# Moving weight loads and casts inside the attention layer of a two-layer decoder trunk

## The chip, the cores and the metric

The kernel runs on one core of a Trainium2 chip. The metric is the device time of one execution in microseconds (us). PE is the matrix engine, DVE the vector engine, ACT the scalar engine, POOL the general one, and SP issues most of the DMAs.

## What is computed

The reference is a trunk of two residual layers over 1024 positions of width 1024, with a final RMS norm. The first layer is a gated linear recurrence; the second, in which the change lies, is causal attention with a forget term, 16 heads of 64:

```python
h = rms_norm(x, norm_g[1])
u = h @ w_in                                  # q, k, v, gate, forget logits
cum = cumsum(log_sigmoid(f_logit + b_f))
logits = q @ k.T / 8 + (cum[q] - cum[k])      # causal
o = softmax(logits) @ v
x = x + (o * silu(gate)) @ w_out
```

All products are done at about float32 precision: each operand is split into a high and a low half, and three matmuls (high x high, low x high, high x low) make one product.

## The kernel before

**Tiling.** In the attention layer the heads come in pairs (128 columns). Each pair needs a K, a Q and a gate (G) projection; each is a *unit* of two halves of 512 positions, and a half is 24 matmuls into one PSUM bank (`gps`), in four steps of six (`gemm_steps`, line 137). Every four heads need 256 columns of V: a *value phase* of 192 matmuls (`vps`), `values`, line 695. The first value group is made before the heads start; groups one to three follow heads 3, 7 and 11.

**Weights.** A unit's weights are two tiles of 128x512 float32, a value group's are four (`in_wv`). SP loads each tile into one of three buffers `wf` (`loaded`, line 114). The cast (`cast16`, line 641) makes the halves in fp16: ACT writes the high half, DVE the low one (line 647), and with that the buffer is free again. The fp16 tiles have eight buffers.

**Scores.** `maxima` (line 925) makes four score blocks of 128 positions for a head and a half `c`: PE writes S; DVE masks it and takes the maximum (line 949); ACT takes the exponential (`p`); DVE the reciprocal of its sum; ACT and DVE write the normalised halves (`pp`, line 963); SP issues a transposing DMA (`pT`, line 966). `weigh` (line 972) multiplies with V into O. `pieces` (line 807) copies K and Q of the head after next into T and U.

**Order.** `run` (line 1018) follows a string for each half of a head: a digit is a step of `weigh` or `maxima`, a dot a step of the *fill*, which plays units (`play`, line 677). At step 0 of a unit's first half `play` loads the next unit's weights and at step 2 of its last half it casts both tiles, behind the last exponential so far (`seen[0]`). When a value phase is due, `run` calls the generator `values` before order places 2 and 5 and at the last score block; after the string the matmuls of the phase run. Each engine's final order is made by a scheduler from these hints, and each engine, SP's queue too, works in its order. The units of the K projection of pairs 3, 5 and 7 are split by a value phase, and their weights are loaded and cast a second time for the second half.

Of the kernel before, what the change touches and what calls it, by code (L numbers as in the profile page):

```python
# [22 lines left out]
KT = 8  # L23
# [12 lines left out]
def f32(ap):  # L36
    return ap.bitcast(F32)
# [3 lines left out]
def trunk(ctx: ExitStack, tc: tile.TileContext, xt, w0, wg, wo0, pc, gn, gf, w1, wv, wf, bf, wo1, out):  # L41
# [26 lines left out]
    def matmul(*args, **kw):  # L68
        pe[0] = nc.tensor.matmul(*args, **kw)  # L69
        return pe[0]  # L70
# [82 lines left out]
    def take(gen, n):  # L153
        for _ in range(n):
            next(gen, None)
# [43 lines left out]
    with nullcontext(ExitStack()) as l0:  # L199
# [8 lines left out]
        def pair():  # L208
            return tuple(hpool.tile([P, HALF], F32R, tag=t, name=t) for t in ("hh", "hl"))
# [33 lines left out]
        first = ([], [])  # L243
        early = [weights(w0[0], lo_eng=nc.vector), weights(w0[NB], lo_eng=nc.gpsimd)]
        k = 0
# [11 lines left out]
        raw = [[pair() for k in range(KT)] for h in range(2)]  # L257
# [321 lines left out]
        for h, cs in enumerate(halves):  # L579
# [4 lines left out]
            for d0 in range(0, KT, 4):  # L584
# [6 lines left out]
                for db, o in enumerate(pts, d0):  # L591
                    mm3(o, wl[db][1], y[1], False, True)
                    x = xs[h][db]
# [26 lines left out]
    with ExitStack() as l1:  # L620
# [11 lines left out]
        seen = [None]  # L632

        def load16(src, shape, b):

            wt = loaded(shape)
            for part, sl in src:
                fetch(wt[:, :, sl], part)
            return wt, b

        def cast16(wt, b):

            n = wt.shape[1]
            both = wpool.tile([P, 2, *wt.shape[1:]], FP16, tag=next(slots), name="w16")
            hi, lo = both[:, 0], both[:, 1]
            cast_last[0] = nc.scalar.activation(hi, wt, AF.Copy, scale=scales[:, b : b + 1])
            nc.vector.scalar_tensor_tensor(lo, wt, scales[:, b : b + 1], hi, ALU.mult, ALU.subtract)  # L647
            return [(hi[:, k], lo[:, k]) for k in range(n)]
# [4 lines left out]
        class Weights:  # L653

            def __init__(self, b):
                self.b, self.raw, self.parts = b, None, None

            def load(self):
                if self.raw is None:
# [1 line left out]
                        load16([(w1[self.b][:, k : k + 4], slice(0, P))], (4, P), 4 + self.b) for k in range(0, KT, 4)  # L661
                    ]

            def cast(self):
                self.load()
                if self.parts is None:
                    self.parts = [x for r in self.raw for x in cast16(*r)]
                return self.parts

        plan = []  # L670

        def job(w, h, start, use):
            u = dict(w=w, h=h, start=start, use=use)
            plan.append(u)
            return u

        def play(units):

            for u in units:
                u["start"]()  # L680
                w, h = u["w"], u["h"]
                after_ = [v["w"] for v in plan[plan.index(u) + 1 :] if v["w"] is not w][:1]
                pt = ps.tile([P, HALF], F32, tag="g", name="gps1")
                for i, _ in enumerate(gemm_steps(pt, zip(w.cast(), hT[h]))):
                    for v in after_ if seen[0] is not None else ():
                        if h == u["first"] and i == 0:
                            v.load()
                        if h == u["last"] and i == 2:
                            with tc.issue_after(seen[0].ins):
                                v.cast()  # L690
                    yield
                nc.vector.scalar_tensor_tensor(pt, pt, unit_w[:, 4 + w.b : 5 + w.b], rs1[h], ALU.mult, ALU.mult)
                u["use"](h, pt)

        def values(g):

            ex = HEADS if g == 0 else 0
            parts, raw = [], []
            for k in range(0, KT, 2):
                src = [(wv[g, :, k : k + 2], slice(0, 256))]  # L700
                if ex:
                    src.append((wf[:, k : k + 2], slice(256, 256 + ex)))
                raw.append(load16(src, (2, 256 + ex), g))
                if k == 2 and not ex:
                    yield
                if k % 4 == 0:
                    continue
                with tc.issue_after(seen[0].ins) if k == 2 and not ex else nullcontext():
                    parts += [x for r in raw for x in cast16(*r)]
                raw = []  # L710
                if k == 2 or not ex:
                    yield
            Vs[2 * g], Vs[2 * g + 1] = [], []
            todo = [(st, k) for st in range(8) for k in range(KT)]
            if not ex:

                todo[: 2 * KT] = [(st, k) for h in range(2) for st in range(2) for k in range(h * 4, h * 4 + 4)]
            pts = {}
            for st, k in todo:
                if k == 0:  # L720
                    if st % 2:
                        pt = ps.tile([P, SEQ], F32, tag="S", name="vps")[:, : 256 + ex]
                    else:
                        pt = ps.tile([P, 256 + ex], F32, tag="g", name="vps")
                    pts[st] = pt
                pt = pts[st]
                c = (st % 4) * P
                xh, xl = hT[st // 4][k]
                wh, wl = parts[k]
                xh, xl = xh[:, c : c + P], xl[:, c : c + P]  # L730
                matmul(pt, xh, wh, start=k == 0, stop=False)
                matmul(pt, xl, wh, start=False, stop=False)
                matmul(pt, xh, wl, start=False, stop=k == KT - 1)
                if k % 4 == 1:
                    yield
                if k < KT - 1:
                    continue
                if ex and st < 4:
                    take(splitting, 2)
                if True:  # L740
                    if ex:
                        nc.vector.tensor_scalar(fz[:, st], pt[:, 256:], rf[:, st : st + 1], None, ALU.mult)
                    for a in range(2):
                        v = vpool.tile([P, 4, HD], FP16, tag=f"v{st}", name=f"v{st}", bufs=2)
                        src = pt[:, a * P : (a + 1) * P].rearrange("p (b d) -> p b d", b=2)
                        rv_ = rv[:, g, st : st + 1]
                        to_hi(v[:, 0::3], src, nc.scalar, scale=rv_)
                        nc.vector.scalar_tensor_tensor(v[:, 1:3], src, rv_, v[:, 0::3], ALU.mult, ALU.subtract)
                        Vs[2 * g + a].append(v)
# [10 lines left out]
        def kq_units(pair, parts):  # L760

            units = []
            for is_k, hs in parts:
                if hs[0] == 0 or pair == 0 or is_k and pair in (3, 5, 7):
                    kqw[is_k] = Weights(is_k * 8 + pair)

                def start(is_k=is_k, first=[True]):
                    if is_k not in kq:
                        kq[is_k] = tuple(
                            kqpool.tile([P, SEQ], F32R, tag=f"qk{p}{is_k}", name=f"qk{p}") for p in "hl"  # L770
                        )

                def use(h, pt, is_k=is_k):
                    cs = halves[h]
                    hi, lo = kq[is_k]
                    if is_k:
                        to_hi(hi[:, cs], pt, nc.scalar)
                        to_lo(lo[:, cs], pt, hi[:, cs], nc.vector)
                    else:
                        to_hi(hi[:, cs], pt, nc.scalar, scale=0.125)  # L780
                        nc.vector.scalar_tensor_tensor(lo[:, cs], pt, 0.125, f32(hi[:, cs]), ALU.mult, ALU.subtract)

                new = [job(kqw[is_k], h, start, use) for h in hs]
                for u in new:
                    u["first"], u["last"] = hs[0], hs[-1]
                units += new
            return units

# [83 lines left out]
        first = values(0)  # L872
# [145 lines left out]
        def run(order, *gens, fill=iter(()), side=iter(()), vals=None):  # L1018

            for n, i in enumerate(order):  # L1020
                if vals and n in (2, 5):
                    with tc.issue_after(turns[-1].ins):
                        next(vals)
                if vals and n == order.rfind("1"):
                    next(vals)
                    behind[:] = loaded_last[0], cast_last[0]
                with tc.issue_after(pe[0].ins):
                    next(fill if i == "." else gens[int(i)], None)
                if i == ".":
                    next(side, None)  # L1030
            for g in gens:
                drain(g)
# [201 lines left out]
        for hd in range(HEADS):  # L1234
            pair = hd // 2
# [21 lines left out]
            first, second = LAST if hd > 11 else ORDER  # L1257
            if hd == HEADS - 1:
                first = "1..1.0.1.0.1..."
# [12 lines left out]
            vals = values(hd // 4 + 1) if hd % 4 == 3 and hd < 12 else None  # L1272
# [91 lines left out]
```

## Time and profile before

| | |
|---|---|
| time, median of 3 runs | 1081.03 us (1080.33 to 1084.85) |
| profiled execution | 1080.8 us, its span 1079.0 us |
| busy | PE 95%, DVE 73%, ACT 61%, POOL 9% |
| transfers | 148.92 MB, 138 GB/s over the span |
| score blocks (S) of the 16 heads | 506.7 to 1037.0 us |
| value phases after heads 3, 7, 11 | from 625.23, 756.33 and 887.66 us |

Busy time is an average over both layers. What a wait of PE costs is read from the timeline: a row there is a group of equal instructions with its start and duration in us, and in brackets the idle time of its engine before it and what ended that. PE's matmuls overlap, so that 24 of them take less than 24 times the duration of one. The granted clock is the share of full speed at which PE may run.

### The profile page before, as it was taken

The page shows a single profiled execution, that of the slowest core. Times are in us where ns is not written, and L with a number is a line of the kernel's source. Part 1 is how long each engine was busy: PE and PEld are TensorE (multiplying, and loading weights), DVE is VectorE, ACT ScalarE, POOL GpSimd, SP SyncE. Part 2 cuts the span into 40 slices and gives each one's busy share as a digit, 9 for nine tenths or more (in the row PEclk, how much of TensorE's full clock was granted, in tenths as well). Part 3 has the DMA queues.
Part 4 walks back from the last instruction along what each step waited for, and adds up shares of the span by engine and source line. Part 5 has one row for each costly group of instructions (what it writes and reads, how often), then busy time and mean ns, then how long its engine had stood idle before and what let it go on. Part 6 is the DMA issues. An engine that isn't in the chain of part 4 may idle for free. (4 is left out here: it accounts for less than half of the span.)

```text
span 1079.0 us, 15071 instructions
## 1 busy us (share of the span) xinstructions
PE 1030.3 (95%) x5094; PEld 722.4 (67%) x5094; DVE 784.9 (73%) x1456; ACT 662.3 (61%) x1211; POOL 92.5 (9%) x87
## 2 busy tenths in 40 slices
PE   9999999999999999998899989999899998999997
PEld 6787878888888888664455465454754546477676
DVE  7789657656956698976878847788387873886675
ACT  8469665656565664757656646666376663764455
POOL 1311011113121110000000000000000000012110
PEclk9999999999999999999999999999999999999999
DMA  6112324233423312534779964978569994689984
GB/s 241 60 49 70 117 88 132 90 106 98 132 84 112 98 56 75 162 96 110 157 155 183 182 160 92 194 165 179 137 111 190 167 185 113 144 185 235 256 200 157
DMA packets 219805, 148.92 MB, mean 138 GB/s; under 512 B 161936, under 2 KB 174864, under 8 KB 219728
## 3 DMA queue, kind: packets, MB, share of 16 engines
q1 hardware_dynamic: 217328, 140.09, 53.7%
q0 software_dynamic: 2400, 7.87, 2.4%
q8 instruction: 40, 0.66, 0.3%
q14 instruction: 37, 0.30, 0.1%
HBM read 73.33 MB, written 11.67 MB: 79 GB/s over the span
## 5 line engine op out<-in xcount | busy, mean ns | idle before, releaser
L69 PE MATMUL gps<-h,w 128*128 128x512 f16 x1152 | 274.5, 384 | 15.5 <-DVE w L647 12.1
L69 PEld LDWEIGHTS <-w 128*128 128x128 f16 x1152 | 105.0, 99 | 145.5 <-issue 17.3
L57 ACT ACTIVATE p<-S,m 128x128 f32<-128x128 f32 (+7 forms) x128 | 94.7, 740 | 72.4 <-DVE m L949 43.1
L57 ACT ACTIVATE pp<-p,sums 128x128 f16<-128x128 f32 (+7 forms) x128 | 96.1, 771 | 36.3 <-DVE sums L961 13.2
L963 DVE SCALAR_TENSOR_TENSOR pp<-p,sums,pp 128x128 f16<-128x128 f32 (+7 forms) x128 | 102.1, 813 | 15.4 <-ACT pp L57 14.7
L69 PE MATMUL S<-T,U 96*128 96x512 f32 (+7 forms) x384 | 108.6, 392 | 2.6 <-ACT p L57 2.2
L69 PE MATMUL vps<-w,h 128*128 128x256 f16 (+1 forms) x768 | 90.5, 277 | 17.9 <-ACT w L57 10.8
L949 DVE CUSTOM_DVE_ANT_0 S<-S,mask 128x128 f32<-128x128 f32 (+7 forms) x128 | 96.9, 759 | 7.9 <-PE S L69 7.3
L110 POOL TENSOR_TENSOR wl<-wf,wh 128x512 fp32r<-128x512 f32 x46 | 71.2, 1552 | 323.1 <-ACT wh L57 264.9
L69 PEld LDWEIGHTS <-h 128*128 128x128 f16 x768 | 75.3, 99 | 32.7 <-issue 14.2
L69 PEld LDWEIGHTS S<-T,U 128*128 128x128 f32 (+1 forms) x384 | 68.9, 191 | 23.9 <-ACT p L57 7.0
L57 ACT CAST wh<-wf 128x512 fp32r<-128x512 f32 x88 | 51.7, 594 | 51.9 <-PE ops L69 26.8
L647 DVE SCALAR_TENSOR_TENSOR w<-wf,wsq,w 128x512 f16<-128x512 f32 (+1 forms) x74 | 54.1, 749 | 33.8 <-ACT w L57 33.6
L69 PE MATMUL ops<-yh,wh 128*128 128x512 f32 x192 | 76.6, 399 | 0.6 <-ACT yh L57 0.5
L69 PE MATMUL ups<-hh,wh 128*128 128x512 f32 x192 | 76.1, 397 | 0.9 <-ACT hh L57 0.8
L69 PE MATMUL ups<-hh,wl 128*128 128x512 f32 x192 | 75.7, 394 | 1.2 <-POOL wl L110 1.2
L69 PE MATMUL ups<-hl,wh 128*128 128x512 f32 x192 | 76.2, 397 | 0.1
L69 PE MATMUL gps<-hh,wh 128*128 128x512 f32 x192 | 75.7, 394 | 0.4 <-ACT wh L57 0.4
L69 PE MATMUL ops<-yh,wl 128*128 128x512 f32 x192 | 75.7, 394 | 0.1
L69 PE MATMUL gps<-hh,wl 128*128 128x512 f32 x192 | 75.5, 393 | 0.0
L69 PE MATMUL gps<-hl,wh 128*128 128x512 f32 x192 | 75.5, 393 | 0.0
L69 PE MATMUL ops<-yl,wh 128*128 128x512 f32 x192 | 74.5, 394 | 0.0
(196 smaller groups left out, 1899.1 us busy)
## 6 DMA issues: line engine op xcount, KB each, us to landing
wf<-in_w SPq DMA_DIRECT2D x106, 256.0 KB
wsf<-in_w SPq DMA_DIRECT2D x48, 256.0 KB
wf<-in_wo SPq DMA_DIRECT2D x64, 128.0 KB
T<-qkh SPq DMA_DIRECT2D x64, 128.0 KB
U<-qkh SPq DMA_DIRECT2D x64, 128.0 KB
x<-in_xt SPq DMA_DIRECT2D x16, 256.0 KB
wsf<-in_wv SPq DMA_DIRECT2D x16, 256.0 KB
x1d<-x SPq DMA_DIRECT2D x16, 256.0 KB
```

The costliest lines, as they stand in the source:

```text
L57: act[0] = op(*args, **kw)
L69: pe[0] = nc.tensor.matmul(*args, **kw)
L110: return eng.tensor_tensor(lo, src, f32(hi), ALU.subtract)
L647: nc.vector.scalar_tensor_tensor(lo, wt, scales[:, b : b + 1], hi, ALU.mult, ALU.subtract)
L949: nc.vector.tensor_tensor_reduce(S[:, :n], S[:, :n], mask[:, SEQ - n :], -1.0, -NEG, ALU.add, ALU.min, accum_out=m)
L963: nc.vector.scalar_tensor_tensor(both[:, :, 1], p, r, both[:, :, 0], ALU.mult, ALU.subtract)
```

## The change

There are three edits. In `values` the first three of the four value tiles of groups one to three are loaded together, before order place 1; the first two are cast before place 5, then the fourth is loaded, and at the last score block the last two are cast. In `play` the next unit's two tiles are cast at steps 1 and 2 (one each) rather than both at step 2. For the K unit that is played just ahead of a value phase the next unit's load moves from step 0 to step 2 and its casts to steps 2 and 3.

```diff
-            def cast(self):
+            def cast(self, n=2):
                 self.load()
-                if self.parts is None:
-                    self.parts = [x for r in self.raw for x in cast16(*r)]
+                while len(self.parts) < 4 * n:
+                    self.parts += cast16(*self.raw[len(self.parts) // 4])
                 return self.parts
...
-            u = dict(w=w, h=h, start=start, use=use)
+            u = dict(w=w, h=h, start=start, use=use, load=0, cast=(1, 2))
...
-                        if h == u["first"] and i == 0:
+                        if h == u["first"] and i == u["load"]:
                             v.load()
-                        if h == u["last"] and i == 2:
+                        if h == u["last"] and i in u["cast"]:
                             with tc.issue_after(seen[0].ins):
-                                v.cast()
+                                v.cast(u["cast"].index(i) + 1)
...
+            else:
+                for k in range(0, 6, 2):
+                    load_v(k)
+                yield
+                with tc.issue_after(seen[0].ins):
+                    cast_v(2)
+                load_v(6)
+                yield
+                cast_v(2)
+                yield
...
+                    if is_k and hs == (0,) and pair in (3, 5, 7):
+                        u["load"], u["cast"] = 2, (2, 3)
...
-                if vals and n in (2, 5):
+                if vals and n in (1, 5):
```

`load_v(k)` loads one value tile (`load16`), `cast_v(n)` casts the next n that are loaded. What the scheduler makes of it is shown at three places.

First ACT ahead of head 11's K unit (`w` are the unit's two fp16 tiles, `pp` the normalised scores, `p` the exponentials). Before:

```order
L57 ACTIVATE p,sums<-S,m 128x1024
L57 ACTIVATE pp<-p,sums 128x7x128
L57 ACTIVATE pp<-p,sums 128x8x128
L57 ACTIVATE yo<-O,wsq 64x512
L57 ACTIVATE p,sums<-S,m 128x128
L57 ACTIVATE w_8098<-wf,wsq 128x512
L57 ACTIVATE w_8101<-wf,wsq 128x512
```

Of the change:

```order
L57 ACTIVATE p,sums<-S,m 128x1024
L57 ACTIVATE w_8065<-wf,wsq 128x512
L57 ACTIVATE pp<-p,sums 128x7x128
L57 ACTIVATE pp<-p,sums 128x8x128
L57 ACTIVATE yo<-O,wsq 64x512
L57 ACTIVATE p,sums<-S,m 128x128
L57 ACTIVATE w_8107<-wf,wsq 128x512
```

The first cast moved ahead of the two normalising activations, the second stayed. DVE's low halves moved in the same way, and the same holds in the other odd heads.

Second SP's queue at the third value phase (`in_wv` value tiles, `in_w` the next unit's, `T` and `U` the copies of K and Q). Before:

```order
L966 DMA_TRANSPOSE pT<-pp 128x2x128
L66 DMA wf<-in_wv 128x512 x2
L966 DMA_TRANSPOSE pT<-pp 128x4x128
L66 DMA wf<-in_w 128x512
L966 DMA_TRANSPOSE pT<-pp 128x6x128
L66 DMA T_4062<-cumd 2x512
L66 DMA T_4062<-qkh 64x512
L66 DMA wf<-in_w 128x512
L66 DMA wf<-in_wv 128x512
```

The fourth value tile comes six rows later. Of the change:

```order
L982 DMA_TRANSPOSE pT<-pp 128x2x128
L66 DMA wf<-in_wv 128x512 x3
L982 DMA_TRANSPOSE pT<-pp 128x4x128
L982 DMA_TRANSPOSE pT<-pp 128x6x128
L66 DMA wf<-in_wv 128x512
L66 DMA T_4062<-cumd 2x512
L66 DMA T_4062<-qkh 64x512
L982 DMA_TRANSPOSE pT<-pp 128x8x128
L66 DMA T_4062<-qkh 64x512
L66 DMA T_4062<-qkl 64x512
L66 DMA wf<-in_w 128x512 x3
```

The first value load stands behind the same transpose as before; the unit's loads moved behind all four value tiles.

Third ACT in the same phase, from the value casts (`w_8144`, `w_8147`, `w_8170` and `w_8173` before, with the unit's `w_8203` and `w_8206` among them) to the copies out of PSUM (`v`). Before:

```order
L57 ACTIVATE w_8144<-wf,wsq 128x512
L57 ACTIVATE w_8147<-wf,wsq 128x512
L57 ACTIVATE w_8170<-wf,wsq 128x512
L57 ACTIVATE w_8203<-wf,wsq 128x512
L57 ACTIVATE w_8173<-wf,wsq 128x512
L57 ACTIVATE w_8206<-wf,wsq 128x512
L57 ACTIVATE yo<-O,wsq 64x512
L57 ACTIVATE v_8276<-vps,rv 128x2x64
L57 ACTIVATE v_8294<-vps,rv 128x2x64
L57 ACTIVATE v_8325<-vps,rv 128x2x64
L57 ACTIVATE v_8279<-vps,rv 128x2x64
```

Of the change, where `w_8146` to `w_8169` are the value tiles:

```order
L57 ACTIVATE w_8146<-wf,wsq 128x512
L57 ACTIVATE w_8149<-wf,wsq 128x512
L57 ACTIVATE w_8166<-wf,wsq 128x512
L57 ACTIVATE w_8169<-wf,wsq 128x512
L57 ACTIVATE yo<-O,wsq 64x512
L57 ACTIVATE w_8203<-wf,wsq 128x512
L57 ACTIVATE v_8276<-vps,rv 128x2x64
L57 ACTIVATE v_8294<-vps,rv 128x2x64
L57 ACTIVATE w_8212<-wf,wsq 128x512
L57 ACTIVATE v_8325<-vps,rv 128x2x64
L57 ACTIVATE v_8279<-vps,rv 128x2x64
```

`v_8276` and `v_8279` are the two copies of the first of the eight blocks, `v_8294` and `v_8325` the first copies of the second and third. The unit's casts moved behind the value tiles and stand among the copies. PE has the same matmuls in both kernels. Of the 192 of a phase the first that needs the third value tile is the 49th before and the 41st now; for the fourth tile it is the 73rd before and the 54th now. The first four blocks are complete after 84, 88, 92 and 96 matmuls before, and after 65, 69, 80 and 96 now.

More of the change, by code (lines that the diff above doesn't have):

```diff
@@ L655, in __init__ @@
             def __init__(self, b):
-                self.b, self.raw, self.parts = b, None, None
+                self.b, self.raw, self.parts = b, None, []
             def load(self):
@@ L698, in values, with load_v @@
             parts, raw = [], []
-            for k in range(0, KT, 2):
+            def load_v(k):
                 src = [(wv[g, :, k : k + 2], slice(0, 256))]
@@ L703, in values, with cast_v @@
                 raw.append(load16(src, (2, 256 + ex), g))
[L704 to L712, printed above, removed]
+            def cast_v(n=1):
+                for _ in range(n):
+                    parts.extend(cast16(*raw.pop(0)))
+            if ex:
+                for k in range(0, KT, 2):
+                    load_v(k)
+                    if k % 4:
+                        cast_v(2)
+                    if k == 2:
+                        yield
+            else:
+                for k in range(0, 6, 2):
+                    load_v(k)
+                yield
[3 more added lines that the diff above has]
+                yield
+                cast_v(2)
+                yield
             Vs[2 * g], Vs[2 * g + 1] = [], []
```

## The prediction

> **What bounds the kernel now.** I read the page first, then the list of waits for PE, then the timeline around the longest of these waits, and last the short windows that show the granted clock.
>
> ```profile
> span 1079.0 us, 15071 instructions
> PE 1030.3 (95%) x5094; PEld 722.4 (67%) x5094; DVE 784.9 (73%) x1456; ACT 662.3 (61%) x1211; POOL 92.5 (9%) x87
> ```
>
> PE is busy for 1030.3 of 1079.0 us. The order printed for the changed kernel holds the same matmuls, so the change can only move PE's idle time and the clock at which PE runs. In the list of waits for PE each row gives total, count and longest, in us:
>
> ```profile
> PE gps L69 <- DVE w L647: 12.1, 8, 2.0
> PE vps L69 <- ACT w L57: 10.8, 8, 2.1
> PE vps L69 <- DVE v L748: 7.0, 6, 1.8
> ...
> PE gps L69 <- ACT w L57: 2.2, 2, 1.9
> PE O L69 <- DMA pT<-pp: 2.0, 2, 1.6
> ```
>
> Two kinds of wait concern the change. In a **value phase** (`vps`: 192 matmuls in a row, three times after the first group) PE waits for cast value tiles, and once for the PSUM copies (L748). At the start of a **unit** (`gps`) it waits for the cast of the unit's own weights. The third value phase shows the first kind; columns are start, duration, engine, line, operation, and in brackets the idle time before it with what ended it:
>
> ```profile
> 882.90 1.05 SPq L66 DMA_DIRECT2D wf<-in_wv  x2
> 886.67 1.37 ACT L57 ACTIVATE w<-wf,wsq 128x512 f16<-128x512 f32 x2 [0.24 <-DMA wf<-in_wv]
> 887.66 5.40 PE L69 MATMUL vps<-w,h 128*128 128x256 f16 x48
> 888.75 0.95 SPq L66 DMA_DIRECT2D wf<-in_w  x1
> 889.80 0.38 SPq L66 DMA_DIRECT2D wf<-in_wv  x1
> 894.04 1.34 ACT L57 ACTIVATE w<-wf,wsq 128x512 f16<-128x512 f32 x2 [6.00 <-DMA wf<-in_wv]
> 894.82 2.78 PE L69 MATMUL vps<-w,h 128*128 128x256 f16 x24 [1.75 <-ACT w L57]
> 895.58 0.33 SPq L66 DMA_DIRECT2D wf<-in_wv  x1
> 898.70 1.34 ACT L57 ACTIVATE w<-wf,wsq 128x512 f16<-128x512 f32 x2 [3.31 <-DMA wf<-in_wv]
> 899.47 2.78 PE L69 MATMUL vps<-w,h 128*128 128x256 f16 x24 [1.87 <-ACT w L57]
> 903.47 2.79 PE L69 MATMUL vps<-w,h 128*128 128x256 f16 x24 [1.22 <-DVE v L748]
> ```
>
> ACT sits idle 6.00 and 3.31 us for value tiles three and four, because their loads were issued only at 889.80 and 895.58: with three load buffers they stood behind the next unit's tiles. The other two phases:
>
> ```profile
> 625.23 5.40 PE L69 MATMUL vps<-w,h 128*128 128x256 f16 x48 [1.55 <-ACT w L57]
> 632.62 4.45 PE L69 MATMUL vps<-w,h 128*128 128x256 f16 x24 [1.99 <-ACT w L57]
> 637.23 2.78 PE L69 MATMUL vps<-w,h 128*128 128x256 f16 x24 [0.16 <-ACT w L57]
> 641.23 10.65 PE L69 MATMUL vps<-w,h 128*128 128x256 f16 x96 [1.22 <-DVE v L748]
> ```
>
> ```profile
> 756.33 5.40 PE L69 MATMUL vps<-w,h 128*128 128x256 f16 x48 [0.58 <-ACT w L57]
> 762.50 2.78 PE L69 MATMUL vps<-w,h 128*128 128x256 f16 x24 [0.77 <-ACT w L57]
> 767.39 2.78 PE L69 MATMUL vps<-w,h 128*128 128x256 f16 x24 [2.11 <-ACT w L57]
> 771.39 3.77 PE L69 MATMUL vps<-w,h 128*128 128x256 f16 x33 [1.22 <-DVE v L748]
> ```
>
> The 24 matmuls at 632.62 took 4.45 us where others take 2.78. The windows tell why; after the span come PE's busy time and, further on, the granted clock:
>
> ```profile
> 629.91:633.32 3.41, 1.42 (x14) 1.11 (x13) 0.71 (x2) 1.34 (x2) 0.00 (x0) 1.00 0.66 169
> 633.32:636.74 3.42, 3.42 (x19) 2.44 (x17) 0.70 (x2) 0.29 (x1) 0.00 (x0) 0.50 0.69 153
> 896.15:899.56 3.41, 1.54 (x15) 1.24 (x13) 0.17 (x2) 0.86 (x2) 0.00 (x0) 1.00 0.86 199
> 899.56:902.98 3.42, 2.69 (x24) 2.16 (x23) 3.36 (x7) 2.83 (x8) 0.00 (x0) 1.00 0.77 237
> ```
>
> A stretch of 3.41 us in which PE is busy for only 1.42 us is followed by 3.42 us at half clock; one with 1.54 us is not. So idle time of about 2 us inside one such stretch costs a second time.
>
> **Value phases: what goes.** The waits after each phase's start are, with 4.45 - 2.78 = 1.67 for the half clock: first 1.99 + 1.67 + 0.16 + 1.22 = 5.04, second 0.77 + 2.11 + 1.22 = 4.10, third 1.75 + 1.87 + 1.22 = 4.84. Together 14.0 us.
>
> **Value phases: what comes.** Tiles one to three are now issued together, so they land one behind the other. The fourth stands next in SP's queue and waits for the buffer of tile one. The load at 888.75 waited for that same buffer, so the fourth can go at 888.75. From issue to cast the rows give 898.70 - 895.58 = 3.1 to 894.04 - 889.80 = 4.2; PE follows the cast by 894.82 - 894.04 = 0.8. That is 892.7 to 893.8. In the new PE order 53 matmuls stand ahead of the first that needs it, 53 x 5.40 / 48 = 6.0 us from 887.66: 893.6. The wait is between nothing and, should a load take 1 us longer than these, 1 us; I take 0.2 a phase, 0.6 in all. Waiting behind this load on SP are the transposed tile and the pieces of T and U, which PE needs only after the remaining matmuls.
>
> The PSUM wait does not vanish, although the first two blocks are now complete after 65 and 69 of the first 96 matmuls. On ACT the first block's second copy stands behind the cast of the next unit's second tile and behind a copy of the third block, complete after 80. With that tile loaded last (issue near 892.5, cast not before 896) the copy ends about where it did. I keep 1.1 of the 1.22 us, 3.3 in all; the ends are 0 and, if these loads come 1 us later, 6.6. The moved unit loads and casts themselves cost nothing else: the last 96 matmuls, 10.65 us, cover them, and without that cover the two casts would cost 1.34.
>
> **The start of a phase does not move.** In SP's new order the first value load stands directly behind the same transpose as before, and the first cast follows its landing (0.24 idle on ACT at 886.67 ended by the DMA). Whatever PE gains just ahead of a phase therefore turns into a longer wait at its start, with a half clock behind it where it passes 2 us. Ahead of the second and third phase PE now waits for a unit's cast:
>
> ```profile
> 747.32 1.25 PE L69 MATMUL gps<-h,w 128*128 128x512 f16 x5 [2.02 <-DVE w L647]
> 748.87 4.06 PE L69 MATMUL gps<-h,w 128*128 128x512 f16 x18
> 877.73 1.25 PE L69 MATMUL gps<-h,w 128*128 128x512 f16 x5 [2.01 <-DVE w L647]
> 879.44 5.57 PE L69 MATMUL gps<-h,w 128*128 128x512 f16 x18
> ```
>
> If these go, the second phase is awaited for 0.58 + 2.02 = 2.6 us, the third for 2.01 + 1.51 = 3.5 (5.57 - 4.06 = 1.51 is its half clock). I charge two half clocks of 1.6 us, 3.2 in all; the ends are none and three (4.8).
>
> The Trainium skill, page "TensorE: Matmul & The Clock Gate", section "Why this matters for your kernels", asks only that idle gaps stay below about 3 us. By that rule the second phase would lose no clock and the sum would be 1.6 us lower. The rows above differ: 1.99 us of idle time already brought 0.50, so the rows decide.
>
> **Units: casts one step apart.** The first cast now stands ahead of two normalising activations, so its DVE half is done before the unit starts. All ten waits of this kind (12.1 + 2.2 = 14.3 us, in eight units) have it on their path. Besides the half clock at 879.44 two more follow them:
>
> ```profile
> 694.76:698.18 3.42, 3.42 (x10) 1.42 (x9) 2.95 (x10) 0.67 (x2) 0.00 (x0) 0.50 0.92 175
> 824.47:827.88 3.41, 3.41 (x9) 1.43 (x9) 2.60 (x8) 0.40 (x1) 0.00 (x0) 0.50 1.10 225
> ```
>
> Three half clocks of 1.5 make 4.5, and 18.8 us at most. How much stays is the unknown. Three of these units stand ahead of value phases and give nothing (above). For the others the score chain on DVE and ACT must keep up:
>
> ```profile
> 701.59 0.76 DVE L692 SCALAR_TENSOR_TENSOR gps<-gps,wsq,rs 128x512 f32<-128x512 f32 x1 [1.44 <-PE gps L69]
> 726.52 2.97 PE L69 MATMUL O<-pT,v 128*128 128x512 f16 x16 [0.37 <-DMA pT<-pp]
> 833.97 0.72 ACT L57 ACTIVATE w<-wf,wsq 128x512 f16<-128x512 f32 x1 [2.47 <-DMA wf<-in_w]
> ```
>
> Behind one of them DVE waits 1.44 us for PE: so much the chain can follow. At 726.52 PE already waits for the chain's transposed tile, so no more stays. In another the chain waits for a load (833.97) and cannot follow. I count 1.44 for three of the five, 4.2 us; the ends are 0 and 18.8.
>
> **Sum.** -14.0 + 0.6 + 3.3 + 3.2 - 4.2 = -11.1. The profiled execution took 1080.8 us (span 1079.0 and 1.8 around it), close to the median of 1081.03. Forecast: 1080.8 - 11.1 = **1069.7 us**.
>
> **Rivals.**
> - *No half clock.* The waits ahead of the phases fall across two stretches, or stay short: 1069.7 - 3.2 = 1066.5. For it: stretches with 1.54 us of work did not trip. Against: 3.5 us hardly splits evenly. Chance 0.12.
> - *The unit gains stay.* PE is the only bound and all 18.8 us hold: 1080.8 - 14.0 + 0.6 + 3.3 - 18.8 = 1051.9. For it: PE's 95%. Against: the wait at 726.52. Chance 0.12.
> - *One wait takes the place of two.* The fourth tile lands late enough for a 2 us wait with its half clock in each phase, 3 x 3.6 = 10.8: 1080.8 - 14.0 + 3.3 + 10.8 - 4.2 = 1076.7. For it: the margin at 893.6 is 0.2 us or less against a slow load. Chance 0.20.
> - *Slower.* In eight heads the early cast delays the two activations behind it, by one cast on ACT (1.37 / 2 = 0.7) and one on DVE (0.7), and through them the transposed tiles that O needs. If all 1.4 us reach O, nothing of the 4.2 stays and 8 x 1.4 = 11.2 is added to -6.9: 1085.1, and 1089.6 with three half clocks. It turns the sign above 6.9 / 8 = 0.9 us a head. Against it: O waits twice in the whole kernel, 2.0 us. Chance 0.06.
> - *The change doesn't do what it says*: the loads do not start earlier at all; this is already in the forecast, as the phase's start.
>
> **How the numbers follow.** The forecast has 0.50, with 1066 to 1074 as its own range. A measurement of this kernel tells about 0.5% (5.4 us) from no change, so faster means below 1075.6. Forecast, first and second rival and a fifth of the third make 0.78 faster; the rest of the third makes 0.16 same; the fourth 0.06 slower. The range 1058 to 1079 leaves out the second rival and the fourth, 0.18.
>
> **What would show it.** Right: in the value phases the ACT waits for value tiles of 6.00 and 3.31 us shrink to one short one, of the 10.8 us of `vps` waits for ACT the 8.7 in the middle of the phases (all but 1.55 and 0.58) nearly vanish while those at the start grow to 6 to 9, the waits of `gps` for L647 nearly vanish, and the waits of S and O for the score chain grow. Wrong: a `vps` wait of 2 us in the middle of a phase (third rival), O waiting in every odd head (fourth), or value phases that begin earlier against the transpose ahead of them.

## The result and the profile after

The changed kernel takes **1066.6 us** (median of 4 runs, 1066.17 to 1067.16) beside 1082.59 of the kernel before on the same chip: ratio **0.9853**, 95% interval 0.9827 to 0.9878, about 16 us less. Its profiled execution has a span of 1065.4 us. Of all executions reported below, one of the six of the kernel with the unit loads not moved ran slow, with 1726.5 us at a granted clock of 0.557, and no ratio includes it.

```profile
span 1065.4 us, 15063 instructions
PE 1028.7 (97%) x5094; PEld 721.8 (68%) x5094; DVE 784.2 (74%) x1456; ACT 659.9 (62%) x1211; POOL 92.2 (9%) x87
```

The list of waits for PE, changed kernel (total, count, longest, in us):

```profile
PE vps L69 <- ACT w L57: 8.3, 3, 3.5
PE O L69 <- DMA pT<-pp: 6.0, 5, 2.0
PE S L69 <- ACT p L57: 4.7, 13, 1.1
```

The waits of `gps` for the units' casts are gone from it, and the waits of `vps` for ACT, eight before, are three. The timeline says which three; PE's rows of the three value phases:

```profile
625.73 10.64 PE L69 MATMUL vps<-w,h 128*128 128x256 f16 x96 [2.66 <-ACT w L57]
637.11 10.65 PE L69 MATMUL vps<-w,h 128*128 128x256 f16 x96 [0.74 <-DVE v L762]
...
750.45 12.31 PE L69 MATMUL vps<-w,h 128*128 128x256 f16 x96 [2.18 <-ACT w L57]
762.95 10.65 PE L69 MATMUL vps<-w,h 128*128 128x256 f16 x96 [0.19 <-DVE v L762]
...
878.28 23.98 PE L69 MATMUL vps<-w,h 128*128 128x256 f16 x192 [3.48 <-ACT w L57]
```

Each phase now waits once, at its start, and then runs through: 96 matmuls take 10.64 us without a break where the copies out of PSUM do not interrupt. The 12.31 and the 23.98 us (twice 10.64 is 21.3) hold half clocks, 1.67 and 2.70 us. The windows around them (span, busy time of PE, of its weight loads PEld, of DVE, ACT and POOL, granted clock, DMA share, GB/s):

```profile
747.64:751.06 3.42, 1.24 (x12) 0.97 (x11) 1.81 (x3) 1.53 (x3) 0.00 (x0) 1.00 1.03 260
751.06:754.47 3.41, 3.41 (x18) 2.37 (x17) 1.56 (x3) 0.99 (x2) 0.00 (x0) 0.50 0.88 188
873.94:877.35 3.41, 0.86 (x7) 0.55 (x6) 1.88 (x3) 0.61 (x1) 0.00 (x0) 1.00 0.54 138
877.35:880.76 3.41, 2.48 (x12) 1.72 (x12) 2.14 (x3) 2.11 (x3) 0.00 (x0) 0.50 0.94 224
880.76:884.18 3.42, 3.42 (x18) 2.35 (x16) 0.84 (x2) 1.40 (x2) 0.00 (x0) 0.50 1.00 216
```

Where the time went is read from the groups of PE's matmuls over the attention layer alone, from the first S matmul to the last (506.7 to 1037.0 us before, 508.3 to 1023.2 after). Behind the second bar stands the idle time ahead of the group. Before:

```profile
L69 PE MATMUL gps<-h,w 128*128 128x512 f16 x1034 | 248.2, 385 | 15.5 <-DVE w L647 12.1 <-ACT w L57 2.2 <-DVE qkl L781 1.2
L69 PE MATMUL S<-T,U 128*128 128x512 f32 (+2 forms) x383 | 108.3, 392 | 2.6 <-ACT p L57 2.2
L69 PE MATMUL O<-pT,v 128*128 128x512 f16 (+2 forms) x368 | 66.9, 326 | 2.1 <-DMA pT<-pp 2.0
L69 PE MATMUL vps<-w,h 128*128 128x256 f16 x576 | 66.5, 277 | 14.4 <-ACT w L57 10.8 <-DVE v L748 3.7
```

After:

```profile
L69 PE MATMUL gps<-h,w 128*128 128x512 f16 x1034 | 242.7, 380 | 1.1 <-DVE qkl L795 1.1
L69 PE MATMUL S<-T,U 96*128 96x512 f32 (+7 forms) x384 | 106.2, 385 | 5.0 <-ACT p L57 4.7
L69 PE MATMUL vps<-w,h 128*128 128x256 f16 x576 | 68.2, 284 | 9.2 <-ACT w L57 8.3 <-DVE v L762 0.9
L69 PE MATMUL O<-pT,v 128*128 128x512 f16 (+2 forms) x368 | 67.0, 326 | 6.0 <-DMA pT<-pp 6.0
```

Idle time falls from 34.6 to 21.3 us (-13.3). Half clocks fall from 6.2 us (1.67 and three of 1.51) to 4.4 (-1.8). Together -15.1; the layer became 530.3 - 514.9 = 15.4 us shorter. The span shows only 13.6, mostly because in this execution the first layer, which has no edit, ended 1.6 us later.

### The profile page after: what moved, and what is told of

The parts are those of the page before. It is cut to its first block, busy times and chain, and to the rows that moved or that the text cites. A ratio compares the mean times of both kernels' runs of the same rounds, so it can differ in the third digit from the quotient of the medians.

```text
span 1065.4 us, 15063 instructions
## 1 busy us (share of the span) xinstructions
PE 1028.7 (97%) x5094; PEld 721.8 (68%) x5094; DVE 784.2 (74%) x1456; ACT 659.9 (62%) x1211; POOL 92.2 (9%) x87
## 2 busy tenths in 40 slices
DMA packets 219805, 148.92 MB, mean 140 GB/s; under 512 B 161936, under 2 KB 174864, under 8 KB 219728
## 5 line engine op out<-in xcount | busy, mean ns | idle before, releaser
L69 PE MATMUL gps<-h,w 128*128 128x512 f16 x1152 | 269.1, 380 | 1.3 <-DVE qkl L795 1.1
L69 PE MATMUL S<-T,U 96*128 96x512 f32 (+7 forms) x384 | 106.2, 385 | 5.0 <-ACT p L57 4.7
L69 PEld LDWEIGHTS <-h 128*128 128x128 f16 x768 | 76.7, 101 | 28.0 <-issue 10.8
L69 PEld LDWEIGHTS S<-T,U 128*128 128x128 f32 (+1 forms) x384 | 67.7, 190 | 28.8 <-ACT p L57 13.6
L69 PE MATMUL O<-pT,v 128*128 128x512 f16 (+3 forms) x396 | 71.0, 322 | 6.0 <-DMA pT<-pp 6.0
```

## Experiments

Idle time by group comes from the same rows of each profile, from its first to its last S; a *half clock* is one stretch of 3.41 us at 0.50 in that layer. Ratios are against the kernel before on the same chip, in five rounds (the changed kernel's first row: the result above).

| kernel | us | ratio [95%] | gps | S | O | vps | half clocks |
|---|---|---|---|---|---|---|---|
| before (profile shown) | 1082.6 | 1 | 15.5 | 2.6 | 2.1 | 14.4 | 4 |
| changed | 1066.6 | 0.9853 [0.9827, 0.9878] | 1.1 | 5.0 | 6.0 | 9.2 | 3 |
| changed, again | 1065.3 | 0.9850 [0.9825, 0.9876] | 1.1 | 4.6 | 5.2 | 8.8 | 1 |
| value tiles only | 1069.4 | 0.9891 [0.9871, 0.9912] | 15.5 | 3.5 | 2.1 | 4.8 | 3 |
| unit casts only | 1076.1 | 0.9972 [0.9958, 0.9986] | 1.1 | 4.6 | 6.0 | 19.0 | 2 |
| unit loads not moved | 1062.7 | 0.9824 [0.9803, 0.9845] | 1.2 | 4.7 | 6.3 | 8.0 | 2 |
| value loads by POOL | 1061.9 | 0.9828 [0.9804, 0.9852] | 1.1 | 6.1 | 12.0 | 0.0 | 1 |
| early loads (0, 3) | 1054.0 | 0.9760 [0.9741, 0.9778] | 1.1 | 4.7 | 5.7 | 1.6 | 0 |
| early (0, 3), casts together | 1067.1 | 0.9874 [0.9852, 0.9896] | 15.4 | 1.3 | 2.0 | 6.7 | 3 |
| early loads (0, 2) | 1055.4 | 0.9764 [0.9743, 0.9785] | 1.1 | 4.7 | 6.2 | 2.6 | 0 |
| early (0, 2), casts together | 1059.9 | 0.9806 [0.9786, 0.9825] | 15.5 | 2.8 | 2.0 | 0.4 | 1 |
| early (0, 3), unit loads not moved | 1056.7 | 0.9773 [0.9753, 0.9793] | 1.2 | 6.5 | 7.8 | 2.5 | 0 |
| early (0, 3), shorter lag | 1059.1 | 0.9815 [0.9796, 0.9834] | 1.1 | 4.1 | 5.6 | 2.2 | 0 |
| early (0, 3), pieces by POOL | 1127.5 | 1.0415 [1.0388, 1.0443] | 1.1 | 4.6 | 62.9 | 0.5 | 17 |

### Each edit alone

Value tiles only (against the changed kernel):

```diff
-            u = dict(w=w, h=h, start=start, use=use, load=0, cast=(1, 2))
+            u = dict(w=w, h=h, start=start, use=use, load=0, cast=(2, 2))
...
-                                v.cast(u["cast"].index(i) + 1)
+                                v.cast(2)
...
-                        u["load"], u["cast"] = 2, (2, 3)
+                        u["load"], u["cast"] = 2, (3, 3)
```

> The changed kernel with both casts of a unit put back to one step (the later of its two steps); the value tiles stay as changed. Theory of the prediction (waits inside the value phases go for good; what PE gains ahead of a phase comes back as a wait for the first value tile, and what it gains ahead of other units is partly taken by the score chain): nearly the whole gain is here. The profile of the changed kernel gives the parts: 14.0 us of waits and half clock inside the three phases went, 0.74 us of the PSUM wait stayed, while of the 18.8 us of unit waits and half clocks 8.3 - 2.1 = 6.2 came back at the phase starts, 4.4 as half clock there and about 5.7 as waits of S and O. So 1082.6 - 13.3 = 1069.3 us, ratio 0.987 to 0.990, the gps waits for L647 back at 10 to 14 us, the vps waits for ACT at 2 to 3 us, no half clock inside the first value phase. Rival, the edits add up independently (each wait removed is time removed): the unit casts were worth 10 us or more of the 16.0, so this kernel keeps 6 us or less, ratio 0.994 or higher.

Unit casts only (against the kernel before; `cast(n)` as in the change):

```diff
-                        if h == u["last"] and i == 2:
+                        if h == u["last"] and i in (1, 2):
...
-                                v.cast()
+                                v.cast(i)
```

> The kernel before with the unit casts alone one step apart; the value tiles as before. Theory of the prediction: the gps waits for L647 (12.1 us) vanish, but the starts of the value phases do not move, so the vps waits for ACT grow by about 6 us at the starts, one to three half clocks of 1.6 us follow them, and S and O wait up to 6 us more for the score chain: a net gain of 1 to 5 us, ratio 0.995 to 0.999, no change that can be told by 0.5%. Rival, the edits add up independently: 10 us or more, ratio 0.991 or lower. Second rival, the early cast delays the normalising activations: slower than before, O waiting in every odd head.

The value tiles alone bring 1.09%, 11.8 us; the unit casts alone 0.28%, 3.0 us. Both numbers lie where the theory put them, and both rivals fall: the unit casts are not worth 10 us, and they do not make the kernel slower. The edits nearly add (14.8 of about 16 us); what the rival had wrong is the size of the second. The list of waits with the unit casts only shows where their 14.4 us of `gps` idle time went:

```profile
PE vps L69 <- ACT w L57: 15.3, 8, 2.7
...
PE O L69 <- DMA pT<-pp: 5.9, 6, 3.3
PE S L69 <- ACT p L57: 4.3, 12, 1.2
```

`vps` for ACT grew from 10.8 to 15.3, O from 2.0 to 5.9, S from 2.2 to 4.3: 10.5 us came back. (This execution took 1074.6 us, 1.5 less than the median, and has two half clocks less than the one before; so its rows show a larger gain than the 3.0 us of the ratio.)

### Does SP's queue hold the start of a phase?

Value loads by POOL, and early loads (both against the changed kernel):

```diff
+                loads_by[0] = nc.gpsimd
                 for k in range(0, 6, 2):
                     load_v(k)
+                loads_by[0] = nc.sync
                 yield
                 with tc.issue_after(seen[0].ins):
                     cast_v(2)
+                loads_by[0] = nc.gpsimd
                 load_v(6)
+                loads_by[0] = nc.sync
```

```diff
-                if vals and n in (1, 5):
+                if vals and n in (0, 3):
```

> The changed kernel, but the value tiles of groups one to three are loaded through POOL's queue in place of SP's; the order on all other engines stays. In the changed kernel PE waits 2.66, 2.18 and 3.48 us at the starts of the value phases for the cast of the first value tile, with 4.4 us of half clock behind the last two, and ACT is idle 1.81, 1.65 and 2.96 us ahead of those casts for the landing. Theory (the first load stands in SP's queue behind a transpose that waits for its scores): with a queue of their own the loads go as soon as their buffer is free, the first casts come earlier by what ACT is idle, 6.4 us in all, the waits at the starts fall to 0.5 to 0.9 each and the half clocks go: 1066.6 - 6.4 - 4.4 = 1055.8, up to 1062 if the score chain takes part of it. Rival, the start hangs on the free buffer or on ACT's order, not on SP's queue: the starts stay, within 2 us of the changed kernel. Second rival, POOL's queue lands its tiles later than SP's: slower than the changed kernel, with ACT waiting longer for value tiles.

> The changed kernel with the three value loads ahead of order place 0 in place of 1, and the fourth tile's load with the first two casts ahead of place 3 in place of 5; all through SP's queue. In that queue the three loads now stand ahead of the pieces of T and of the first transpose of the half, so at the third phase they can be issued near 868.7 in place of 872.63 us. Theory (SP's queue sets the start of a phase): the first cast comes earlier by the idle time of ACT ahead of it (1.81, 1.65, 2.96 us), the half clocks of 4.4 us go, the fourth tile is still in time (issue near 876 at the earliest, needed at 881): 1056 to 1062 us. Rival, what is moved behind the three loads (pieces of T, transposes) becomes late in its turn: O or S wait 2 to 3 us more in heads 4, 8 and 12, and the time stays within 3 us of the changed kernel.

Yes. With a queue of their own PE waits 0.0 us for value tiles, and with early loads 1.4. The third phase with early loads, from PE's and SP's rows:

```profile
859.80 1.81 SPq L66 DMA_DIRECT2D wf<-in_wv  x3
...
867.72 0.59 SPq L66 DMA_DIRECT2D wf<-in_wv  x1
...
865.47 5.79 PE L69 MATMUL vps<-w,h 128*128 128x256 f16 x50
871.95 15.69 PE L69 MATMUL vps<-w,h 128*128 128x256 f16 x142 [0.68 <-ACT w L57]
```

The loads go 5.7 us before PE's first matmul of the phase, against 878.28 - 872.63 = 5.65 with 3.48 us of idle PE among them in the changed kernel; the phase starts without a wait, and no stretch of the whole layer runs at half clock. The 1054.0 us are the fastest median of the study, 2 us better than the 1056 to 1062 expected and some 10 us (0.9853 to 0.9760) better than the changed kernel. In this phase PE still waits 0.68 us for the fourth tile. The rival, that what stands behind the three loads becomes late, falls (O 5.7 against 6.0, S 4.7 against 5.0).

POOL's queue removed the same wait, but its 1061.9 us are the upper end of what was expected. Its groups:

```profile
L69 PE MATMUL S<-T,U 96*128 96x512 f32 (+7 forms) x384 | 106.3, 386 | 6.1 <-ACT p L57 5.8
L69 PE MATMUL O<-pT,v 128*128 128x512 f16 (+2 forms) x368 | 68.7, 331 | 12.0 <-DMA pT<-pp 9.5 <-DMA T<-qkh 2.5
L69 PE MATMUL vps<-w,h 128*128 128x256 f16 x576 | 63.4, 273 | 0.0
```

O's idle time doubled: 2.60, 1.87 and 2.51 us of it stand directly ahead of the three phases. Ahead of the first, POOL issues value tiles at 609.70 and 615.45 us, while SP issues the last two transposes of the half between 610.75 and 616.66, and O waits for them until 620.7. With early loads SP issues these transposes from 610.29 to 615.68 and the tiles from 615.73 on, and O waits 0.2 us.

### Are the unit casts worth more when the starts can move?

Both casts of a unit back in one step (as in *value tiles only*), once with `n in (0, 3)` and once with `n in (0, 2)`; and `(0, 2)` by itself.

> The kernel with the early value loads (places 0 and 3), with both casts of a unit put back to one step. With the value loads at their places in the changed kernel, spreading the unit casts was worth 2.8 us (1069.4 against 1066.6). Theory (the gain of the unit casts was eaten at the starts of the value phases, which could not move): with the starts free to move, the same edit is worth what the unit waits and their half clocks cost, 18.8 us, less the 5.7 us by which S and O wait more for the score chain, so about 13: this kernel takes 1064 to 1068 us, close to the 1069.4 of the late loads, because ahead of the phases it has nothing to gain. Rival, the unit casts are worth little by themselves (the score chain takes nearly all of it): 1055 to 1058 us, 1 to 4 above the 1054.0 of the early loads.

> Early value loads with the fourth tile's load and the first two casts ahead of place 2 in place of 3. SP's queue then has the fourth load ahead of the second transpose of the half in place of behind it. The fourth tile was in time already (vps waits for ACT 1.4 us in all), so no change: 1052 to 1056 us. Rival, the load holds up the second transpose, and O waits more for its tile: 1055 to 1060.

> The same with both casts of a unit put back to one step. With the fourth load ahead of place 3 that took 1067.1 us, but of the 13.1 us against the early loads only a part was the unit casts: PE waited 2.2 us in the middle of each value phase for the fourth tile (vps waits for ACT 6.7 us against 1.4) with one half clock of 1.67. Theory (with starts free to move the unit casts are worth 14.2 us of gps waits and two half clocks, 3.2, less 7.3 us of waits of O and S, so about 10): with the fourth load earlier these 7 us go and 8 to 10 us above the kernel with the early loads remain, 1060 to 1064. Rival, the unit casts are worth no more than the 2.8 us of the late starts: 1055 to 1058.

The 1067.1 us of the first lie inside the theory's range, but not for its reason. The first half of its first value phase:

```profile
624.01 3.88 PE L69 MATMUL vps<-w,h 128*128 128x256 f16 x34
...
630.04 10.12 PE L69 MATMUL vps<-w,h 128*128 128x256 f16 x76 [2.16 <-ACT w L57]
```

The fourth tile came too late by 2.2 us in each phase. Its load was hardly the reason: it was issued at 626.07, 2.06 us after the phase's first matmul, and with early loads 2.55 us after it (623.22 and 620.67). But with the casts together the scheduler also gave PE another order: 34, 30 and 30 matmuls stand ahead of the wait for that tile, where with early loads 50 do. So this run changes more than the unit casts. With place 2, which by itself changes nothing that can be told (1055.4 against 1054.0), the wait is gone, and 4.5 us are left between casts together (1059.9) and apart (1055.4). With the late starts the same edit is worth 0.9891 - 0.9850, 4.4 us. By the intervals of the ratios each of these differences is uncertain by about 3 us. So the theory that the starts ate the gain of the unit casts **falls**: no difference shows between starts that can move and starts that can't, and the 8 to 10 us expected did not come. The rival's 2.8 us is not excluded, although all four executions (1058.6 to 1060.8) lie above its 1055 to 1058. What the starts no longer take, others do: of 14.4 us of `gps` idle time S and O take 6.1 (5.4 with late starts), `vps` 2.2 (4.4), and the kernel with casts together has one half clock to lose here, not three. These rows alone would leave 7.6 us, more than the 4.5 measured; where the rest went stays open.

### The moved unit loads, and what is left for O

```diff
-                    if is_k and hs == (0,) and pair in (3, 5, 7):
-                        u["load"], u["cast"] = 2, (2, 3)
```

> The changed kernel without its third edit: the K unit ahead of a value phase loads the next unit's tiles at step 0 and casts them at steps 1 and 2 like any other unit. SP's queue then has one of these loads directly behind the fourth value tile and one two rows later, ahead of most pieces of T. Theory (the fourth value tile is still ahead of them, and the wait for the PSUM copies is the only thing that the move could change): within 1.5 us of the changed kernel's 1066.6, the 0.74 us of PSUM wait in the first phase gone or up to 1.2 in each phase. Rival, the move is what makes room for the fourth value tile: PE waits 1 to 2 us for it in each phase, half clocks behind some, 1069 to 1077 us.

> The changed kernel itself once more, for a comparison with the three others of this chip: 0.983 to 0.988 of the kernel before.

> The kernel with early value loads (places 0 and 3) without the third edit: the K unit ahead of a value phase loads and casts the next unit's tiles as any other unit does. Without that edit the changed kernel took 1062.7 us beside a kernel before of 1080.5 (0.9824), with it 1066.6 beside 1082.6 (0.9853); the intervals overlap. Theory (the move of the unit's loads is worth nothing): within 3 us of the early loads' 1054.0. Rival one, the move costs about 4 us by itself: 1050. Rival two, the move makes room for the fourth value tile: now that the phases start earlier, that tile lands 1 to 2 us late in each, 1058 to 1062.

The third edit brings nothing that can be told: without it 0.9824 against 0.9850 with it (2.8 us, more than the 1.5 expected, though the intervals overlap), and with early loads 0.9773 against 0.9760 and 0.9764. The rivals in which the fourth tile needs room from it (1069 us or more, 1058 or more) fall, and so does the one in which the move costs 4 us with early loads (1050 expected, 1056.7 measured).

Pieces of T and U by POOL, and a shorter lag (both against early loads):

```diff
+                loads_by[0] = nc.gpsimd if hd < 13 else nc.sync
                 piece(f32(to), from_, lag)
+                loads_by[0] = nc.sync
```

```diff
-        def pieces(hd, is_k, c, lag=3):
+        def pieces(hd, is_k, c, lag=2):
```

> The kernel with the early value loads, with the pieces of T and U of heads below 13 issued through POOL's queue in place of SP's. In the kernel with early loads O still waits 5.7 us for transposed tiles and S 4.4 us for exponentials. In the changed kernel's head 6 the scores of the transpose that O waited for (2.01 us) were ready at 713.46 us, and the transpose was issued at 716.17 behind an earlier transpose and a piece of T. Theory (SP's queue is what makes these transposes late): with the pieces out of it the transposes go 1 to 2 us earlier, the waits of O fall by half or more, 1049 to 1052 us. Rival, transposes and other transfers slow each other whatever queue they stand in, as the value tiles on POOL's queue did (O waited 2.6, 1.87 and 2.51 us ahead of the phases): the waits of O stay or grow, 1054 to 1060 us.

> The kernel with the early value loads (places 0 and 3), with the pieces of T and U placed behind the last transpose but one in place of the last but two; SP's queue stays the only one. What is left of O's waits there is 5.7 us, the longest (1.36 us) in head 6: the transpose of 128x16x128 was issued at 711.08, behind that of 128x14x128 (708.41) and a piece of T (710.54). With the shorter lag the two transposes follow each other without the piece. Theory (the order in SP's queue makes these transposes late): the waits of O fall to 4 us or less, the longest under 1 us, apart from the 1.8 us of the last heads; 1050 to 1053 us. Rival, the transposes wait for each other and for their scores, whatever stands between them: O waits 5 to 7 us as before, and where pieces of T or U are now later, S waits more; 1053 to 1058 us.

In both runs the theory falls that the pieces in SP's queue make the transposes late. With the pieces on POOL's queue the kernel is 4% slower than before and 7% slower than with early loads, far beyond the rival's range. One of its waits of O, 8.0 us long, in windows and in SP's rows:

```profile
560.00:564.00 4.00, 3.81 (x22) 1.98 (x20) 3.70 (x9) 3.95 (x8) 2.27 (x5) 1.00 1.17 210
564.00:568.00 4.00, 4.00 (x20) 1.93 (x20) 3.94 (x10) 1.48 (x5) 2.05 (x4) 1.00 1.15 189
568.00:572.00 4.00, 1.78 (x9) 0.59 (x6) 3.25 (x12) 3.13 (x9) 0.03 (x1) 1.00 1.11 136
572.00:576.00 4.00, 0.00 (x0) 0.00 (x0) 1.42 (x3) 1.07 (x2) 0.00 (x0) 0.61 1.20 136
```

```profile
562.42 10.70 SPq L984 DMA_TRANSPOSE pT<-pp  x2
573.21 0.74 SPq L66 DMA_DIRECT2D wf<-in_w  x1
574.12 2.97 SPq L984 DMA_TRANSPOSE pT<-pp  x2
```

POOL is busy 2.27 and 2.05 us issuing pieces, the DMA share stays at 1.1 to 1.2 for all 16 us (the times of packets are added, so it can pass 1), and PE stands still in the last 4. Two transposes hold SP's queue for 10.70 us; with early loads the two at the same place, from 560.71 us, take 4.04. The transposes that O waits for stand behind them and are issued only from 574.12. So SP's order still counts; what the second queue changed is how long its transposes take. The reading, which no run tests by itself, is that the transposes share the DMA engines with pieces that nobody waits for yet. With the shorter lag O waits 5.6 us as with the longer one. In head 6 the two transposes do follow each other without the piece, but from 709.00 to 713.95 us where with the longer lag they and the piece took 708.41 to 713.84, and O waits 1.65 us there in place of 1.36. So the piece is not what makes them late, and what does stays open. The waits fit the rival; the time of 1059.1 us is 1.1 above its range. With the shorter lag the profiled execution took 1052.6 us and the five others 1058 to 1061; what these met is in no trace.

## Why the prediction held, step by step

The forecast was 1069.7 us, the result 1066.6, inside its own range of 1066 to 1074 but only 0.6 us from the lower end. The gain was further off than the time: 11.1 us forecast, 16.0 measured. The forecast started from 1080.8 us, and the median of the kernel before beside the result was 1082.6. In the terms of the sum, by the profiled execution:

| step | forecast | measured |
|---|---|---|
| waits inside the phases | -14.0 | -14.0 |
| fourth tile | +0.6 | 0 |
| PSUM copies | +3.3 | +0.9 |
| unit waits with their half clocks | -18.8 | -18.8 |
| come back at the starts, as waits | +6.8 | +6.2 |
| half clocks at the starts | +3.2 | +4.4 |
| taken by S and O | +7.8 | +6.3 |
| sum | -11.1 | -15.0 |

(The forecast gave the last four as +3.2 and -4.2: it took the three units ahead of the phases, 5.3 us of waits and 1.5 of half clock, as lost at the starts, and of the other 12.0 us kept 4.2. That 4.2 is a slip: three times 1.44 is 4.3.) By edit the forecast was 14.0 - 0.6 - 3.3 = 10.1 us for the value tiles and 4.2 - 3.2 = 1.0 for the unit casts; alone they brought 11.8 and 3.0.

**The waits inside the phases go: right.** None is left. The fourth tile's load was issued at 879.04, 0.76 us after the start of the third phase, and its cast began at 882.55, 4.3 us after it. The forecast of 5.0 to 6.1 us is for PE, 0.8 behind the cast, so it puts the cast at 4.2 to 5.3: it came at the early end. PE ran at half clock here, which would hide a late tile; in the first phase it did not, and there the cast began 4.6 us after the start (630.36 and 625.73) without a wait. The third phase:

```profile
872.63 2.82 SPq L66 DMA_DIRECT2D wf<-in_wv  x3
877.51 2.11 ACT L57 ACTIVATE w<-wf,wsq 128x512 f16<-128x512 f32 x3 [2.96 <-DMA wf<-in_wv]
...
879.04 0.33 SPq L66 DMA_DIRECT2D wf<-in_wv  x1
882.55 0.72 ACT L57 ACTIVATE w<-wf,wsq 128x512 f16<-128x512 f32 x1 [2.94 <-DMA wf<-in_wv]
```

ACT's wait of 6.00 us for a value tile is 2.94. The rival of one wait in place of two did not come.

**The PSUM copies: the term with the largest error**, 3.3 forecast, 0.74 + 0.19 measured. It depends on the unit's second cast meeting the copies. Three profiles show it without and with half clocks: 0.71, 1.28 and 0.58 with the value tiles only (no half clock in a phase); 0.74 in the phase without a half clock, 0.19 and 0 in the two with one; and in the changed kernel's second profile the other way round, 0 in the first phase, which had the half clock, and 1.24 and 0.77 in the others. The reading is that a phase slowed at its start gives the copies time, so that this wait and the half clock stand in for each other, where the forecast charged both. It rests on these profiles and is not shown. It is not the whole, either: with early loads and with POOL's queue no phase has a half clock in it, and the copies cost 0.2 us or less. In the third phase with early loads ACT makes three copies ahead of the unit's first cast (873.37 to 874.61, the cast at 876.26); in the changed kernel that cast (886.09) is ahead of all copies (from 888.44).

**The start does not move: right.** Its waits were forecast at 2.6 us in the second phase and 3.5 in the third, and measured at 2.18 and 3.48. In the first phase, for which the forecast gave no number, it grew from 1.55 to 2.66, by about the 1.23 us that PE had waited for a unit's cast at 615.25. Early loads show the cause: SP's order.

**Half clocks: two forecast, two measured**, but the second is two stretches long (3.2 us forecast, 4.4 measured). The wait of 2.18 us fell into one stretch, with 1.24 us of work left in it. The number of stretches changes from execution to execution: three stretches in the first profile of the changed kernel, one in the second (1061.1 us). By the Trainium skill, page "TensorE: Matmul & The Clock Gate", section "Why this matters for your kernels", idle gaps need only stay below about 3 us. The trace differs: 2.18 us cost clock here.

**The unit gains: the size was between the rivals, as forecast.** S and O took 6.3 us in place of 7.8. That it came so close is partly luck: the 1.44 us for three of five units was a guess from one row of DVE, and no run measures it. O waits in five places and not in every odd head; the rival of a slower kernel fell.

## What to carry to other kernels

A wait removed ahead of a stage whose first load has a fixed place in an in-order queue comes back at that stage: move that load too (some 10 us here, where the unit casts brought 3 to 4.5). Where a kernel's traffic is dense, a second queue is no free path: an order that keeps loads behind the transfers that are needed next was worth more than a queue without waits. Where two waits may cover each other, such as a slow start and a late copy behind it, ask whether both can occur before both are charged.

## What the runs showed of the hardware

The clock goes by stretches of 3.413 us that run on at a fixed pace: the first three half clocks of the kernel before begin at 633.32, 694.76 and 824.47 us, 18 and 38 such stretches apart. The border of idle time beyond which the clock halves lies near 1.9 us within one stretch, and is not sharp. Over the attention layers of all 14 profiles, the 17 stretches at full clock with 1.3 us of PE work or less were all followed by a half clock, and of the some 2000 with 1.6 us or more none was; of the 22 between (1.38 to 1.56 us) half were. In the kernel with early loads at (0, 3) and casts together a stretch with 1.56 us of PE work was followed by half clock, and a later one with 1.49 us was not:

```profile
514.45:517.87 3.42, 1.56 (x9) 1.16 (x7) 3.39 (x10) 2.15 (x5) 0.00 (x0) 1.00 0.45 90
517.87:521.28 3.41, 3.12 (x8) 1.39 (x8) 3.12 (x6) 2.55 (x5) 0.00 (x0) 0.50 0.76 167
814.83:818.24 3.41, 1.49 (x8) 0.67 (x5) 3.31 (x8) 2.65 (x7) 0.00 (x0) 1.00 1.03 228
818.24:821.66 3.42, 3.31 (x16) 1.59 (x17) 3.42 (x12) 0.56 (x3) 0.00 (x0) 1.00 0.96 177
```

A half clock goes on when its own stretch has too little work: 2.48 us of it, in the changed kernel at 877.35, were followed by a second such stretch; 2.82 us, with the unit loads not moved at 622.84, and 3.12 us above were not.

Transposes came later when other transfers stood on a second queue: O waited 12.0 us in place of 6.0 with twelve value tiles on POOL's queue, and 62.9 us in place of 5.7 with the pieces there. The Trainium skill, page "DMA: Bandwidth & Descriptors", section "Rules for kernel authors", says that spreading transfers over the issuing engines gains no bandwidth, since they share the same DMA engines; these runs agree: with the pieces on POOL's queue the same 148.92 MB moved at 132 GB/s over the span, and with early loads at 142. Here the second queue cost time as well, 0.9760 to 1.0415 of the kernel before.
